# Probes of a segment mean sent as pieces of two rows between the data tiles

One core of a Trainium2 chip. The metric is the device time of one execution in microseconds (us). A profile's span is some 1.8 us shorter than the time of the same run.

## The reference

```python
def setup_inputs():
    n = 10_000_000
    num_segments = 10000
    return {
        "data": np.random.randn(n).astype(np.float32),
        "segment_ids": np.sort(np.random.randint(0, num_segments, n)),
    }

def reference(data, segment_ids):
    num_segments = int(segment_ids.max()) + 1
    sums = np.zeros(num_segments, dtype=np.float32)
    counts = np.zeros(num_segments, dtype=np.float32)
    np.add.at(sums, segment_ids, data)
    np.add.at(counts, segment_ids, 1)
    return sums / np.maximum(counts, 1)
```

The ids are sorted and a segment has about 1000 elements, so a piece of 875 neighbours rarely holds more than one boundary between segments.

## The kernel before

The 10 million elements are laid out as 128 partitions of 78125. A partition is cut into 90 rows of 875. In each row the kernel must find the position of the boundary, if there is one, and split the row's sum there.

It does not read all the ids. Every 175th id is read as a **probe** (five per row, each a transfer element of its own, 8 bytes). A **first look** (VectorE) finds between which two probes the boundary lies. A **gather** (issued by GpSimd) fetches the 175 ids there. Their sum (ScalarE, `add_ids`) gives the exact position in the **second look** (VectorE). Then VectorE sums the part of the row in front of the boundary (`split`) while ScalarE sums the whole row (`total`). The work goes in groups of six rows. These are the parts that matter here; bodies are cut where marked.

```python
L, S, K = 875, 175, 5            # row, distance of probes, probes per row
GROUPS = [6] * 15
X_PROBE, X_DATA, X_LOOK = 11, 26, 9
RING = 18                        # rows of gathered ids that fit

def load_probes(g):
    a = 0 if g == 0 else K * bounds[g] + 1
    b = min(K * bounds[g + 1] + 1, NPR)
    nc.sync.dma_start(out=pr_flat[:, a:b], in_=ids_p[:, a * S : (b - 1) * S + 1 : S])

def load_data(t):                # a tile is two rows; 18 buffers
    d = dpool.tile([P, 2 * L], FP32, name="data_t")
    ...
    nc.sync.dma_start(out=d[:, 0 : c - a], in_=data_p[:, a:c])

def first_look(g):               # five small VectorE steps
    ...                          # v.tensor_reduce(out=SG[:, a:b], in_=pr32[:, a:b, ...]) and so on
    gather(g)                    # six indirect transfers, one per row

def add_ids(r):                  # ScalarE; runs six rows ahead of total(r)
    nc.scalar.activation(out=junk_a[:, 0:W], in_=gt32[:, r % RING, ...], func=ACT.Copy, accum_out=GS[:, r : r + 1])

# where the steps are put: behind the split of row r on VectorE
put(a - 1, second_look(a, b))                             # just ahead of its group
put(max(bounds[g] - X_LOOK, 0), first_look(g), 5)         # nine rows ahead of its group

# the order of the data queue, and the main loop
for r in range(-X_PROBE - X_DATA, NR):
    while pnext < NG and bounds[pnext] <= r + X_PROBE + pnext // (NG - 1) + X_DATA:
        load_probes(pnext)
        pnext += 1
        if pnext == 1:
            load_data(0)
            nt = 1
    while nt < NT and 2 * nt <= r + X_DATA:
        load_data(nt)
        nt += 1
    ...
    while r >= -1 and gs < NR and gs <= r + x_sum(gs):
        add_ids(gs)
        gs += 1
    if r >= 0:
        total(r)
        split(r)
        for f in after[r]:
            f()
```

Probes and tiles share one queue, issued by SyncE and served in order. In the long run it reads: one group of probes (30 per partition, 3840 elements of 8 bytes), three tiles, one group of probes, and so on. Gathers have a queue of their own on the same 16 DMA engines.

## Time and profile before

| | kernel before |
|---|---|
| time, median of 3 | 189.86 us (189.63 to 189.91) |
| profiled run | 192.2 us |
| busy: VectorE, ScalarE, GpSimd | 140.9, 136.5, 99.8 us |
| VectorE's waits for data tiles | 6.0 us, 6 waits |
| ScalarE's waits for gathers | 37.0 us, 22 waits |
| last full tile landed (from the trace) | 176.0 us |

The profiled run was 2.3 us slower than the median, so its absolute times have to be taken with care. A second profile of the same kernel, among the experiments, took 190.58 us with a span of 188.7, and its last full tile landed at 174.5 us. Below, "before" in comparisons of traces is this second one.

A word on reading: the DMA share of a window is the time in which packets were open, summed over engines. Two queues on one engine, or a packet that is open but waits for its bytes, both raise it, so it can pass 1.00 and hides losses. The GB/s beside it is the safer column.

Three words recur. A **burst** is one group's probes on end in the queue. A **hold** is the time for which an issue instruction of the sync engine does not finish. A **descriptor** is one element of a transfer as one DMA engine sees it: a piece of two rows is 81 of them per engine (80 probes and one that tells of completion), a tile 9.

### The profile page before, as it was taken

The page shows a single profiled execution, that of the slowest core. Times are in us where ns is not written, and L with a number is a line of the kernel's source. Part 1 is how long each engine was busy: PE and PEld are TensorE (multiplying, and loading weights), DVE is VectorE, ACT ScalarE, POOL GpSimd, SP SyncE. Part 2 cuts the span into 40 slices and gives each one's busy share as a digit, 9 for nine tenths or more (in the row PEclk, how much of TensorE's full clock was granted, in tenths as well). Part 3 has the DMA queues.
Part 4 walks back from the last instruction along what each step waited for, and adds up shares of the span by engine and source line. Part 5 has one row for each costly group of instructions (what it writes and reads, how often), then busy time and mean ns, then how long its engine had stood idle before and what let it go on. Part 6 is the DMA issues. An engine that isn't in the chain of part 4 may idle for free.

```text
span 190.2 us, 1434 instructions
## 1 busy us (share of the span) xinstructions
PE 1.6 (1%) x6; PEld 1.4 (1%) x6; DVE 140.9 (74%) x438; ACT 136.5 (72%) x362; POOL 99.8 (52%) x119
## 2 busy tenths in 40 slices
PE   0000000000002000000000000000000000010000
PEld 0000000000001000000000000000000000010000
DVE  6521295969478792956978999566899969999991
ACT  8011498995989499698685948959868594999930
POOL 5577875065753737266272572726638278782000
DMA  6999999999999999999999999999999999999100
GB/s 29 174 188 414 271 330 413 174 405 261 331 412 176 401 284 297 412 147 374 311 284 408 138 370 339 266 392 186 401 301 274 299 349 412 397 405 399 54 0 8
DMA packets 70163, 54.61 MB, mean 287 GB/s; under 512 B 60016, under 2 KB 60584, under 8 KB 70151
## 3 DMA queue, kind: packets, MB, share of 16 engines
q1 hardware_dynamic: 64219, 40.50, 73.0%
q0 software_dynamic: 5760, 14.01, 23.2%
q14 instruction: 12, 0.10, 0.2%
q10 hardware_dynamic: 172, 0.00, 0.1%
HBM read 56.59 MB, written 0.04 MB: 298 GB/s over the span
## 4 chain that ended last, share of the span: by engine, by line
DMA 45%; issue 27%; ACT 9%; POOL 8%; DVE 7%; POOLq 0%; ACTq 0%; DVEq 0%
DMA GT<-in_segment_ids_dram,IDX 23%; DMA data_t<-in_data_dram 22%; POOL GT L304 7%; ACT junk_a L334 5%; ACT junk_a L314 4%; DVE junk_v L339 2%; DVE jj L235 1%; POOL i_i L197 0%; POOLq L304 0%; DVE most L744 0%; DVE add L736 0%; DVE PS L561 0%; DVE add L744 0%; DVE ps L558 0%; DVE most L750 0%
## 5 line engine op out<-in xcount | busy, mean ns | idle before, releaser
L304 POOL DMA_INDIRECT GT<-in_segment_ids_dram,IDX x90 | 90.9, 1010 | 70.1 <-ACT junk_a L314 28.1
L339 DVE SCALAR_TENSOR_TENSOR junk_v<-iota,q,data_t 128x875 bf16<-128x875 f32 x90 | 100.4, 1116 | 7.4 <-DMA data_t<-in_data_dram 6.0
L334 ACT ACTIVATE junk_a<-data_t 128x875 bf16<-128x875 f32 x90 | 83.6, 929 | 3.5 <-ACT junk_a L314 0.7
L314 ACT ACTIVATE junk_a<-GT 128x175 bf16<-128x175 int32 x90 | 32.4, 361 | 41.9 <-DMA GT<-in_segment_ids_dram,IDX 37.0
L321 DVE SCALAR_TENSOR_TENSOR q<-YY,GS 128x6 f32<-128x6 f32 (+1 forms) x19 | 3.2, 171 | 27.1 <-ACT junk_a L314 18.2
L314 ACT ACTIVATION_READ_ACCUMULATOR junk_a<-GT 128x1 f32 x90 | 16.8, 186 | 0.0
L334 ACT ACTIVATION_READ_ACCUMULATOR junk_a<-data_t 128x1 f32 x90 | 16.8, 186 | 0.0
L339 DVE DVE_READ_ACCUMULATOR junk_v<-iota,q,data_t 128x1 f32 x90 | 7.4, 82 | 0.0
L271 DVE TENSOR_REDUCE SG<-pr 128x6 f32<-128x30 int32 x15 | 2.7, 180 | 5.4 <-DMA pr<-in_segment_ids_dram 5.3
L186 ACT ACTIVATE GT<-q 128x3150 int32<-128x3150 f32 x1 | 3.0, 2998 | 0.0
L280 DVE TENSOR_SCALAR far<-ST 128x6 f32<-128x6 f32 x15 | 2.6, 171 | 0.5
L287 DVE SCALAR_TENSOR_TENSOR IDX<-ST,wb 128x6 int32<-128x6 f32 (+2 forms) x16 | 2.6, 165 | 0.5
L274 DVE SCALAR_TENSOR_TENSOR ST<-pr,SG 128x6 f32<-128x6 int32 x15 | 2.5, 165 | 0.5
L283 DVE TENSOR_TENSOR ST<-ST,far 128x6 f32<-128x6 f32 x15 | 2.5, 165 | 0.5
L290 DVE SCALAR_TENSOR_TENSOR YY<-ST,SG 128x6 f32<-128x6 f32 x15 | 2.4, 158 | 0.0
L235 DVE CAST jj<-jj_i 128x128 f32<-128x128 int32 x1 | 1.5, 1484 | 0.7 <-POOL jj_i L234 0.7
L186 ACT ACT_TABLE_LOAD x1 | 1.3, 1283 | 0.7 <-PEq L894 0.7
L703 POOL TENSOR_SCALAR pb<-pb 128x168 f32<-128x168 f32 (+1 forms) x2 | 1.6, 784 | 0.2
L589 DVE TENSOR_TENSOR_SCAN FFP<-NBP,FFP,XX 128x16 f32<-128x16 f32 (+2 forms) x4 | 1.5, 382 | 0.0
L543 PE MATMUL badp<-bads,ones 128*128 128x1 f32 x2 | 0.6, 362 | 106.3 <-DVE bads L542 106.3
L583 DVE TENSOR_TENSOR q<-T,q 128x44 f32<-128x44 f32 (+3 forms) x4 | 0.7, 180 | 0.9 <-DVE RB L574 0.4
L736 POOL TENSOR_TENSOR xa<-pa,RG 128x528 f32<-128x528 f32 x1 | 1.2, 1247 | 0.2 <-DVE RG L733 0.2
(129 smaller groups left out, 44.3 us busy)
## 6 DMA issues: line engine op xcount, KB each, us to landing
data_t<-in_data_dram SPq DMA_DIRECT2D x44, 875.0 KB
GT<-in_segment_ids_dram,IDX POOLq DMA_INDIRECT x90
data_t<-in_data_dram SPq DMA_DIRECT2D x1, 437.5 KB
pr<-in_segment_ids_dram SPq DMA_DIRECT2D x13, 30.0 KB
data_t<-in_data_dram SPq DMA_DIRECT2D x1, 125.0 KB
out_dram<-OUT SPq DMA_DIRECT2D x1, 36.6 KB
pr<-in_segment_ids_dram SPq DMA_DIRECT2D x1, 31.0 KB
pr<-in_segment_ids_dram SPq DMA_DIRECT2D x1, 26.0 KB
```

Of the source, the lines that this page charges most:

```text
L186: nc.scalar.activation(out=gt32[:, :, 0 : 2 * W : 2], in_=view(q5[:, 0, 0:1], [[0, RING], [0, W]]), func=ACT.Copy)
L235: nc.vector.tensor_copy(out=jj, in_=jj_i)
L271: v.tensor_reduce(out=SG[:, a:b], in_=pr32[:, a:b, 0 : 2 * K : 2], axis=AX.X, op=ALU.add)
L274: v.scalar_tensor_tensor(out=ST[:, a:b], in0=VI[:, a + 1 : b + 1], scalar=float(K), in1=SG[:, a:b], op0=ALU.mult, op1=ALU.subtract,)
L280: v.tensor_scalar(out=far, in0=ST[:, a:b], scalar1=0.0, scalar2=FAR, op0=ALU.is_equal, op1=ALU.mult)
L283: v.tensor_add(out=ST[:, a:b], in0=ST[:, a:b], in1=far)
L287: v.scalar_tensor_tensor(out=IDX[:, c:d], in0=ST[:, c:d], scalar=float(w), in1=wb[:, c:d], op0=ALU.mult, op1=ALU.add)
L304: nc.gpsimd.indirect_dma_start(out=GT[:, r % RING, :], out_offset=None, in_=ids2d[:], in_offset=bass.IndirectOffsetOnAxis(ap=IDX[:, r : r ...
L314: nc.scalar.activation(out=junk_a[:, 0:W], in_=gt32[:, r % RING, 0 : 2 * W : 2], func=ACT.Copy, accum_out=GS[:, r : r + 1],)
L321: nc.vector.scalar_tensor_tensor(out=KK[:, a:b], in0=YY[:, a:b], scalar=float(S // K), in1=GS[:, a:b], op0=ALU.mult, op1=ALU.subtract,)
L334: nc.scalar.activation(out=junk_a[:, 0:n], in_=d, func=ACT.Copy, accum_out=t)
L339: nc.vector.scalar_tensor_tensor(out=junk_v[:, 0:n], in0=iota[:, 0:n], scalar=KK[:, r : r + 1], in1=d, op0=ALU.is_lt, op1=ALU.mult, accum_ ...
```

## The change

The probes of a group go out as three transfers of two rows, with a tile between one piece and the next. The last piece of a group stands where the whole group stood, so the first look has its probes no later than before. The intent is to take the long run of small elements apart, so that the data queue never has 240 of them on end in front of a tile.

```diff
-X_PROBE = 11
+X_PIECE = 15
+PIECE = 2
...
-    def load_probes(g):
-        a = 0 if g == 0 else K * bounds[g] + 1
-        b = min(K * bounds[g + 1] + 1, NPR)
+    def load_probes(r0, r1):
+        a = 0 if r0 == 0 else K * r0 + 1
+        b = min(K * r1 + 1, NPR)
...
-    for r in range(-X_PROBE - X_DATA, NR):
-        while pnext < NG and bounds[pnext] <= r + X_PROBE + pnext // (NG - 1) + X_DATA:
-            load_probes(pnext)
-            pnext += 1
-            if pnext == 1:
+    for r in range(-X_PIECE - X_DATA, NR):
+        while pnext < NR and pnext <= r + X_PIECE + pnext // bounds[NG - 1] + X_DATA:
+            n = GROUPS[0] if pnext == 0 else PIECE
+            load_probes(pnext, pnext + n)
+            if pnext == 0:
                 load_data(0)
                 nt = 1
+            pnext += n
```

## The prediction

> **What bounds the kernel now.** I read the page first (busy shares, slices, queues), then who waited for whom, then the chain of work that ended last, then the sync engine's part of the timeline, and last windows around one burst of probes. On the page:
>
> ```profile
> DVE  6521295969478792956978999566899969999991
> ACT  8011498995989499698685948959868594999930
> DMA  6999999999999999999999999999999999999100
> GB/s 29 174 188 414 271 330 413 174 405 261 331 412 176 401 284 297 412 147 374 311 284 408 138 370 339 266 392 186 401 301 274 299 349 412 397 405 399 54 0 8
> q1 hardware_dynamic: 64219, 40.50, 73.0%
> q0 software_dynamic: 5760, 14.01, 23.2%
> ```
>
> The 16 DMA engines look full until about 175 us of 190.2, but the bytes swing between about 412 GB/s and dips of 138 to 188. A dip comes once per group: 57216 of the 64219 packets on q1 are 8-byte probes, 30 per partition and group. So the transfers are one bound. They are not the only one:
>
> ```profile
> ACT junk_a L314 <- DMA GT<-in_segment_ids_dram,IDX: 37.0, 22, 8.6
> ...
> DVE q L321 <- ACT junk_a L314: 18.2, 8, 3.6
> ...
> DVE junk_v L339 <- DMA data_t<-in_data_dram: 6.0, 6, 1.9
> ```
>
> VectorE waits only 6.0 us for data, all of it after 88 us (rows 38, 44, 50, 56, 68, 72). Its larger wait is for ScalarE's sums of gathered ids, and ScalarE waits 37.0 us for gathers. The chain alternates between the two:
>
> ```profile
> 59.67 7.07 DMA GT<-in_segment_ids_dram,IDX
> ...
> 85.58 13.21 DMA data_t<-in_data_dram
> ...
> 119.86 7.37 DMA GT<-in_segment_ids_dram,IDX
> ...
> 155.22 19.10 DMA data_t<-in_data_dram
> ```
>
> The gather part is a loop, read off the timeline. After the second look of group g (63.12 us) VectorE does four rows (4.9 us), then the first look of g+2 (68.01); 1.75 us later the first gather of g+2 is issued (69.76). A gather's sum runs 6.3 to 8.3 us after its issue, and six rows at ScalarE's pace of 1.54 us lead to the next second look (85.86). Two groups take 22.7 us, or about 11 us per group. The measured mean is (85.9 - 22.4) / 6 = 10.6 us up to 85.9 us, with no data wait at all, and (143.6 - 85.9) / 5 = 11.5 us after it, where the data waits lie.
>
> **What a burst of probes costs today.** Windows of the burst at 57 us (start:end, span, then busy us of each engine; the last two columns are the DMA share and GB/s):
>
> ```profile
> 57.00:60.00 3.00, 0.59 (x3) 0.63 (x4) 2.86 (x12) 2.90 (x8) 0.33 (x1) 1.00 1.23 155
> 60.00:61.00 1.00, 0.39 (x3) 0.30 (x2) 0.96 (x3) 0.97 (x3) 0.69 (x2) 1.00 0.90 154
> 61.00:67.00 6.00, 0.00 (x0) 0.00 (x0) 4.36 (x16) 3.19 (x10) 4.78 (x5) 1.00 0.99 389
> ```
>
> The second line is the interesting one: the probes are done at 60.2 us, yet the next 1 us moves 154 GB/s where 389 follow. The share of 0.90 hides this, because the first data packets after a burst are open for long without moving. The cause shows in the sync engine's issues:
>
> ```profile
> 84.78 0.70 SPq L162 DMA_DIRECT2D pr<-in_segment_ids_dram  x1
> ...
> 85.58 10.04 SPq L170 DMA_DIRECT2D data_t<-in_data_dram  x1
> ```
>
> The data tile behind each group of probes is held at issue 9.4 to 10.8 us, in eleven of the twelve groups sent from 12 us on (7.4 us in the last), even for tiles whose buffer was never used before; so it isn't a buffer. It is let go only when the probes ahead are nearly drained (holds end at 36.33, 59.58 and 83.72 us, the last probes of these bursts start 0.58, 0.55 and 0.75 us later, but for a straggling engine at 37.4). Its first packet starts 0.6 us later, its sixteenth 1.0 to 1.3 us later. Engines that had finished their probes are starved meanwhile. At 83.72 us one engine alone still had 99 probes to start while 15 had posted their completion; I read this as room for about 100 to 128 descriptors per engine between the issue and the data movers (an estimate). From the bytes of each 3 us window after a burst, taking 7000 bytes at 266 ns and a probe at 9 ns, the lost time is 0.5 to 1.3 us per burst, some 10 us in all.
>
> **What the skill says.** The Trainium skill, "DMA: Bandwidth & Descriptors", section "Rules for kernel authors", says that a strided last dimension becomes one descriptor per element, and that many small transfers should be joined, those under 64 KB being mostly overhead. The first agrees (57216 packets of 8 bytes). The second speaks against the change: 30 KB transfers become 10 KB. In "Queues, rings and completion order" the page says that an engine alternates between queues packet by packet; the trace agrees: where a gather is active, probes fall from 544 starts in 0.2 us (all 16 engines) to under 100. In "Latency and other measured facts" it gives about 0.6 us to the first byte on this path; the trace shows the same 0.6 us between the end of a hold and the first packet. That latency matters only when nothing is queued ahead of it.
>
> **The change part by part.** Removed: 14 issues of 26 or 30 probes per partition. Added: 42 of 10 (the last is shorter), so 28 issues more. At 0.65 us each (median of L162) they cost SyncE 18 us, off the path: it holds still about 10 us of every 12 anyway. VectorE's first look depends on three transfers instead of one; such a wait is 21 ns where it stands alone in this trace, 2 x 14 x 21 ns = 0.6 us at most. Completion packets: 28 x 16 of about 9 ns over 16 engines, 0.25 us. Probes and bytes are unchanged, and the last piece of a group is where the whole group was, so no first look starts later for it (first looks wait 5.3 us for probes, all before 14 us).
>
> Moved: per engine a piece is 80 probes and a completion, 81 descriptors, and a tile 9. Together 90, which fits into the 100 to 128 estimated above, where 241 did not. So the tile behind a piece should be queued before the piece starts, and most of the next piece while the tile takes its 2.1 us (8 packets of 266 ns). The starved 0.5 to 1.3 us should shrink to a fraction. I take 0.7 us off each of 13 bursts, or 9 us less transfer time, with the last data landing near 166 us instead of 175.
>
> What reaches the end is less. Only waits for data can shrink: of the 6.0 us, 0.5 + 1.9 + 0.6 us (rows 44, 56, 68) lie on the loop that leads from the second look at 75.0 us to ScalarE's last wait at 159.4; the wait of 1.5 us before row 72 partly runs beside it. From 159.4 ScalarE runs without a pause to 183.2 and the end follows 3 us later, so a gain ahead of 159.4 passes through whole. That is 3.0 + about 0.7 = 3.7 us. Against it: gathers now have uncontested engines during the starved gaps, and will share them with data instead. A sum starting 0.1 us later per gather loop over some 7 two-group loops costs 0.7 us; waits above, 0.3 us. Sum: 189.86 - 3.7 + 1.0 = 187.2, which I round to 187.0.
>
> **Rivals.** (a) Room for only about 64 descriptors: then each tile waits behind its piece as it does behind a group today and there are three gaps for one, up to 2 x 13 x 0.8 = 20 us more transfer time. For it: holds that end 0.55 us before a burst ends fit about 60 probes at 9 ns. Against it: the 99 probes on one engine at 83.72 us, and 81 on average per engine at the hold's end at 151.75. Time 195 to 205; I give it one in ten. (b) The transfers are the true bound from end to end: the chain gives them 45% and they run at 0.99 share. Then all 9 us come back: 181. Against it: the loop takes 10.6 us per group even before 85 us, where data is never late, and there earlier data gains nothing. (c) The gathers are slowed more than I allow, since the gaps close in their favour no longer: 0.4 us per loop would cost 3 us and give 189 to 190. For it: a sum follows its gather's issue by 4 us where the first gather meets a burst (row 48: 4.0, row 54: 3.6) and by about 7 where it meets data (row 30: 7.2). This is the most serious one.
>
> **Range and chances.** Between (b) in part and (c): 183.0 to 191.5. The line of 2% is 186.06, just below my value. Faster by over 2% 0.33, within 2% 0.55, slower by over 2% 0.12, of which most is (a).
>
> **What would show it.** Right: the GB/s row has no dips under 230 after 20 us, the 10 us holds of L170 become many short ones, VectorE's wait for data falls under 2 us, the data queue ends before 170 us, and ScalarE's wait for gathers stays at 34 to 41 us. The step on room is wrong if a low-byte gap follows every piece. The step on the loop is wrong if ScalarE's wait for gathers changes by more than 5 us, or if the end moves as far as the last data does.

## The result

The changed kernel took 188.80 us (188.19 to 189.03, 4 runs); the kernel before, in the same rounds, 189.88 (189.63 to 190.22). The ratio is 0.9937, with a 95% interval from 0.9907 to 0.9966. Ratios here are the mean time of one kernel's fast runs over that of the other's of the same rounds, so they are not quite the ratio of the medians quoted. The result is correct.

187.0 us was forecast, so the time lies inside the range, but the gain is 1.1 us where the working gave 2.7 (189.86 to 187.2, which was rounded to 187.0). The profile of the changed kernel is that of its quickest run (188.19 us, span 186.4). Its page, slices of the span with GB/s:

```profile
DMA  6999999999999999999999999999998999999000
GB/s 28 178 178 340 331 325 328 306 341 330 316 330 319 338 333 305 326 335 332 314 310 335 318 328 317 329 344 307 326 246 246 343 405 406 405 406 391 15 0 12
```

The same row of the second profile of the kernel before:

```profile
GB/s 28 176 141 386 357 244 403 231 308 395 212 406 247 351 394 236 407 208 407 311 280 402 189 392 292 268 390 219 401 284 292 283 347 415 401 404 398 63 0 9
```

The dips are gone: from the fourth slice to the last probes, before swung between 189 and 407, and now the queue runs at 305 to 344 GB/s, with one exception, two slices of 246 at 135 to 144 us. Who waited for whom:

```profile
ACT junk_a L315 <- DMA GT<-in_segment_ids_dram,IDX: 35.9, 24, 6.4
...
DVE q L322 <- ACT junk_a L315: 21.7, 10, 6.9
DVE junk_v L340 <- DMA data_t<-in_data_dram: 6.7, 12, 0.8
```

And in the second profile of the kernel before:

```profile
ACT junk_a L314 <- DMA GT<-in_segment_ids_dram,IDX: 38.1, 23, 8.1
...
DVE q L321 <- ACT junk_a L314: 25.0, 10, 7.6
...
DVE junk_v L339 <- DMA data_t<-in_data_dram: 7.3, 6, 2.0
```

The waits for data did not go away. They are twice as many and shorter (0.8 us at most, where it was 2.0), and in sum 6.7 us. Sync engine's issues in the timeline (start, duration, what):

```profile
65.98 2.46 SPq L171 DMA_DIRECT2D data_t<-in_data_dram  x1
68.49 0.68 SPq L163 DMA_DIRECT2D pr<-in_segment_ids_dram  x1
69.21 2.57 SPq L171 DMA_DIRECT2D data_t<-in_data_dram  x1
```

One hold of ten microseconds per group has become one of 2 to 5 us per tile, which is about the pace at which the queue drains a tile and a piece. And the chain:

```profile
57.77 6.46 DMA GT<-in_segment_ids_dram,IDX
...
103.30 6.19 DMA GT<-in_segment_ids_dram,IDX
...
111.47 7.40 DMA data_t<-in_data_dram
...
129.50 10.82 DMA data_t<-in_data_dram
...
160.93 6.87 DMA GT<-in_segment_ids_dram,IDX
```

Data takes 10% of it and gathers 23%; in the second profile of the kernel before they take 16 and 27%, in the first 22 and 23%. The last full tile landed at 171.8 us, 2.7 us before the 174.5 of the kernel before. The 2.7 us are themselves unsure: they compare a run of 188.19 us with one of 190.58, and in a kernel further down (g3_only, a run of 188.32 us) this tile lands at 171.8 us with a single group in pieces. But the gaps did close, and the transfers did not end 9 us earlier. That is the first thing to explain.

**Why closed gaps gave so little.** Five windows of the changed kernel have nearly no gather in them; three of them (columns as in the prediction):

```profile
69.00:72.00 3.00, 0.00 (x0) 0.00 (x0) 1.64 (x5) 2.87 (x9) 2.39 (x3) 1.00 1.11 321
81.00:84.00 3.00, 0.00 (x0) 0.00 (x0) 1.66 (x6) 2.88 (x9) 2.23 (x3) 1.00 1.09 314
114.00:117.00 3.00, 0.00 (x0) 0.00 (x0) 1.50 (x4) 2.87 (x9) 2.39 (x3) 1.00 1.10 313
```

All five together (57 to 60, 69 to 72, 81 to 84, 114 to 117, 126 to 129) last 15 us; the tiles in them move 312 GB/s, with the probes it is 317. At 7000 bytes per 266 ns on each of 16 engines (421 GB/s) the bytes need 11.1 us. The other 3.9 us went to 403 probes per engine, counted in the trace: 9.6 ns each. In the fastest stretches of a burst of the kernel before, with probes queued and no gather beside them, 544 probes started per 0.2 us, which is 5.9 ns each on an engine. So, as an estimate from these fastest stretches, a group's 240 probes cost 240 x 5.9 ns = 1.4 us and a gap before, and 240 x 9.6 ns = 2.3 us without a gap after. A whole burst is not that fast: with gathers beside it for a part of its time, its middle 90% took 2.07 us on average. Over the whole stretch from 20 us to the last probe, gathers and tiles both taken at 26 bytes per ns and engine, all else counted to the probes, six rows cost 2.84 us before and 2.72 after. The saving is 0.1 us per group by this count, where I had taken 0.7. The count differs between profiles of one kernel (the first profile of the kernel before gives 3.0 us), so the saving may be 0.1 to 0.3 us, but not 0.7.

### The profile page after: what moved, and what is told of

It reads as the page before. It is cut to its first block, busy times and chain, and to the rows that moved or that the text cites. A ratio compares the mean times of both kernels' runs of the same rounds, so it can differ in the third digit from the quotient of the medians.

```text
span 186.4 us, 1479 instructions
## 1 busy us (share of the span) xinstructions
PE 1.6 (1%) x6; PEld 1.4 (1%) x6; DVE 140.8 (76%) x438; ACT 136.6 (73%) x362; POOL 99.9 (54%) x119
## 4 chain that ended last, share of the span: by engine, by line
DMA 33%; issue 32%; ACT 14%; POOL 13%; DVE 4%; POOLq 1%; ACTq 0%
DMA GT<-in_segment_ids_dram,IDX 23%; POOL GT L305 12%; DMA data_t<-in_data_dram 10%; ACT junk_a L335 9%; ACT junk_a L315 5%; POOLq L305 1%; DVE jj L236 0%; POOL i_i L198 0%; DVE junk_v L340 0%; DVE most L745 0%; DVE add L737 0%; POOL pb L703 0%; DVE sel L648 0%; DVE most L751 0%; POOL KL L689 0%
## 5 line engine op out<-in xcount | busy, mean ns | idle before, releaser
L315 ACT ACTIVATE junk_a<-GT 128x175 bf16<-128x175 int32 x90 | 32.4, 360 | 38.1 <-DMA GT<-in_segment_ids_dram,IDX 35.9
L236 DVE CAST jj<-jj_i 128x128 f32<-128x128 int32 x1 | 0.8, 840 | 0.7 <-POOL jj_i L235 0.7
L571 DVE RECIPROCAL ct<-ct 128x16 f32<-128x16 f32 (+2 forms) x4 | 1.2, 300 | 0.1
L544 PEld LDWEIGHTS badp<-bads,ones 128*128 128x128 f32 x2 | 0.5, 310 | 104.8 <-DVE bads L543 104.8
```

## The experiments

I had two theories. A: the loop of looks, gathers and sums holds the end, and eats what the transfers save. B: the transfers hold the end alone and save little. The edits are given against the kernel before or the changed kernel. The medians of the kernel before lay between 189.1 and 190.7 us (the chip was not always the same). Five of the experiments had slow executions (strict, after_look12, split_only and piece3 one each, after_early two of six, its profiled one among them); the ratios leave these out, the medians quoted contain them.

**A second profile of the kernel before** (no edit).

> The kernel before, unchanged, to get a profile in the fast state: the one that the prediction was read from took 192.2 us where the median is 189.9, and was marked slow. If the slow state made the gap between the two profiles (3.8 us of span) larger than the one between the medians (1.1 us), this profile shows a span near 188 and the last data landing 1 to 2 us earlier than the 176 us seen. If the profile was typical, the span is 190 again.

Measured: 190.58 us (one run, so its state is unknown), span 188.7, last full tile at 174.5, waits of VectorE for data 7.3 us, of ScalarE for gathers 38.1. So part of the distance between the first two profiles was the slow run. The shape was typical: dips down to 141 to 250 GB/s once per group.

**No two pieces in a row.**

```diff
-        while pnext < NR and pnext <= r + X_PIECE + pnext // bounds[NG - 1] + X_DATA:
+        while pnext < NR and pnext <= r + X_PIECE + X_DATA:
```

> The changed kernel, but the pieces of the last group come one row later, so that no two pieces follow each other (in the changed kernel two do, near 135 to 140 us, and 1.2 to 1.8 us of transfer time are lost there). Theory (room for about 100 descriptors per engine, gaps where probes exceed it): the low stretch at 138 to 141 us disappears, no window of 3 us between 20 and 145 us moves under 240 GB/s, and the last data land 1 to 1.5 us earlier. Time: if transfers set the end, 187.4 (1.3 us less than the changed kernel); if the loop of gathers sets it, 188.6 to 188.9, the same.

Measured: 188.48 us (188.28 to 188.80 for the five fast runs; the sixth was slow at 191.27), ratio 0.9936 [0.9891, 0.9980]. Windows of the changed kernel and of this one around the place where two pieces followed each other:

```profile
138.00:141.00 3.00, 0.00 (x0) 0.00 (x0) 2.96 (x8) 2.81 (x9) 2.39 (x3) 1.00 0.83 110
```

```profile
138.00:141.00 3.00, 0.00 (x0) 0.00 (x0) 2.95 (x5) 2.83 (x8) 2.39 (x3) 1.00 1.03 305
```

The hole is filled. Two pieces on end, 162 descriptors per engine, bring a gap; one piece and a tile do not. But the last full tile landed only 0.6 us earlier (171.2; 1 to 1.5 were expected) and the time is the same: the better end of the queue did not reach the end of the kernel.

**The loop relieved, first try.** In both kernels first looks and probes were moved three rows ahead: `first_look(g)` put at `max(bounds[g] - X_LOOK - 3, 0)`, and `X_PROBE` 14 or `X_PIECE` 18.

> The kernel before with the first look, and so the gathers, of groups 3 to 13 three rows earlier, and the probes three rows earlier too, so that the loop of looks, gathers and sums has some 3.6 us more room per two groups. Theory A (the loop holds the end, the transfers hold it second): ScalarE's wait for gathers falls from 37 us to under 20 us, VectorE's wait for data rises over 10 us, time 186.5 to 188.5. Theory B (the transfers hold the end alone): time within 0.6 us of before, 189.3 to 190.5, with waits only moved from gathers to data.

> The changed kernel with first looks and probes three rows earlier. Theory A (the loop eats the transfer time that the change saves): with the loop out of the way the whole saving shows, 3 to 5 us under the same edit of the kernel before, 183 to 185. Theory B (transfers hold the end alone, and the change saves little of them): 188 to 189, about 1 us under the same edit of the kernel before.

Measured: before with it 190.98 us, ratio 1.0080 [1.0026, 1.0133]; changed kernel with it 190.76, ratio 1.0002 [0.9933, 1.0071]. ScalarE's wait for gathers fell to 16.1 and 15.7 us, VectorE's for data rose to 24.2 and 24.4, and ScalarE, which had hardly waited for data, now did for 22.4 and 23.3. Both times lie above what either theory had forecast. The waits only moved from gathers to data, which is nearer to theory B. But the edit also put more probes in front of the first tiles, so it is not clean.

**Less data.** In both kernels a tile is loaded without its last 125 columns, and the second row is read 125 columns earlier. All sums keep their size; the result is wrong.

```diff
-        nc.sync.dma_start(out=d[:, 0 : c - a], in_=data_p[:, a:c])
+        c2 = c - 125 if t < NT - 1 else c
+        nc.sync.dma_start(out=d[:, 0 : c2 - a], in_=data_p[:, a:c2])
...
-        d = tiles[r // 2][:, (r % 2) * L : (r % 2) * L + n]
+        o = (r % 2) * (L - 125 if r < NR - 2 else L)
+        d = tiles[r // 2][:, o : o + n]
```

> The kernel before with 1/14 less data moved: each tile of two rows is loaded without its last 125 columns (6500 bytes per partition for 7000), and the second row is summed from column 750 on instead of 875. All sums keep their sizes, probes and gathers are untouched; the result is wrong on purpose. If the transfers hold the end: 8 packets x 44 tiles x 19 ns (1/14 of 266 ns) = 6.7 us less, 182 to 184 us, and the span still ends 14 to 15 us after the last full tile. If the loop of looks, gathers and sums holds it: at most 1.5 us less, 188 to 189.6.

> The changed kernel with the same 1/14 less data (wrong result on purpose). Transfers hold the end: 6.7 us under the changed kernel, 181 to 183, and still about 1 us under the same cut of the kernel before. Loop: 187 to 188.8.

Measured: before with less data 188.75 us (188.15 to 189.21), ratio 0.9950 [0.9895, 1.0005]; changed with less data 186.73 (186.35 to 187.06), ratio 0.9841 [0.9788, 0.9894]. In the kernel before the last full tile landed at 167.4 us, 7.1 us earlier than at 174.5, and the end moved by 0.9 us. Its waits, with no wait for data among them:

```profile
ACT junk_a L315 <- DMA GT<-in_segment_ids_dram,IDX: 36.9, 21, 7.8
DVE q L322 <- ACT junk_a L315: 29.0, 10, 7.5
```

So theory B falls as well: with no wait for data left, the loop alone takes nearly as long. And here the two kernels are 2.0 us apart, with no overlap of their runs, though VectorE and ScalarE wait for data in neither. The changed kernel's 186.73 us lie just under the 187 to 188.8 that were forecast for a loop that holds the end. Its waits:

```profile
ACT junk_a L316 <- DMA GT<-in_segment_ids_dram,IDX: 28.9, 19, 4.2
DVE q L323 <- ACT junk_a L316: 27.8, 10, 6.7
...
ACT junk_a L316 <- DVE IDX L289: 6.4, 1, 6.4
```

**Both reliefs, and a cleaner one.** First looks three rows earlier, probes left where they were.

```diff
-            put(max(bounds[g] - X_LOOK, 0), first_look(g), 5)
+            put(max(bounds[g] - X_LOOK - 3, 0), first_look(g), 5)
```

> The kernel before with the first looks of groups 3 to 13 three rows earlier, probes where they were. Theory (two bounds of nearly one height: with less data the kernel before still took 188.75 us, so its loop alone gives about that, and the transfers alone give about 189): VectorE's wait for data rises over 12 us, time 188.5 to 190.5. Rival (the loop was the one bound, and the earlier probes spoiled the first try at this): 186 to 187.5.

> The changed kernel with the same edit. Two bounds: 186.5 to 188.5 (its last data land some 3 us earlier than before's, so the transfers alone would give 186 to 187), VectorE's wait for data over 10 us. Rival: 184 to 185.5.

> Both reliefs at once in the kernel before: 1/14 less data (wrong result on purpose) and first looks three rows earlier. Two bounds of one height: each relief alone gave 1 us or nothing, both give at least 4 us, 181 to 185. Rival (a third thing, the pace of ScalarE and VectorE themselves, holds the end): as with the cut alone, 188 to 189.

> Both reliefs at once in the changed kernel. Two bounds: 179 to 183, at least 3 us under the cut alone (186.7). Rival (pace of the engines): 186 to 187.

Measured, with the earlier runs, as ratios to the kernel before of the same rounds (median of all runs in us, 95% interval):

| | kernel before | changed kernel |
|---|---|---|
| as it is | 1 | 0.9937 (188.80) [0.9907, 0.9966] |
| less data | 0.9950 (188.75) [0.9895, 1.0005] | 0.9841 (186.73) [0.9788, 0.9894] |
| earlier looks | 0.9870 (187.74) [0.9790, 0.9950] | 0.9886 (188.42) [0.9808, 0.9963] |
| both | 0.9596 (182.94) [0.9515, 0.9677] | 0.9626 (182.91) [0.9550, 0.9703] |

The forecast for the kernel before with earlier looks was missed: 187.74 us lies under the 188.5 to 190.5 of two bounds and nearer to the 186 to 187.5 of the loop as the one bound, and VectorE's wait for data is 7.6 us and not over 12 (ScalarE's is 19.6). The other three of these four runs lie in the ranges of two bounds, and it is the row with both reliefs that speaks for them.

Three things can be read from the table. Less data alone gives the kernel before half a per cent, earlier looks alone 1.3, both 4: there are two bounds of nearly one height, and lifting one uncovers the other. With the looks earlier, the two kernels can't be told apart, with all data as well as with less: in the mean of the fast runs the changed kernel is 0.3 us slower with all data (give or take 0.9, an estimate from their scatter) and 0.2 us slower with less. With less data and the looks where they were, they are 1.1% apart. So what the change wins there, it wins in the loop, and its saving of transfer time does not show where transfers matter most.

Why not? I compared the 1.2 us after a burst in five bursts of the kernel before, without and with earlier looks. Without:

```profile
72.40:73.60 1.20, 0.00 (x0) 0.00 (x0) 0.00 (x0) 1.17 (x3) 0.90 (x2) 1.00 0.98 160
83.70:84.90 1.20, 0.00 (x0) 0.00 (x0) 0.85 (x2) 1.17 (x4) 0.91 (x1) 1.00 0.99 172
```

With:

```profile
73.00:74.20 1.20, 0.00 (x0) 0.00 (x0) 0.00 (x0) 1.14 (x5) 0.00 (x0) 1.00 1.05 286
84.30:85.50 1.20, 0.00 (x0) 0.00 (x0) 0.00 (x0) 1.14 (x5) 0.00 (x0) 1.00 1.03 248
```

The mean of the five is 183 GB/s without and 292 with. By packets, over all twelve bursts, gathers move about 107 GB/s in this time without and 213 with; data 60 and 44. With the looks earlier, gathers are under way when the tile behind the probes is late, and use the engines. Six rows of probes then cost 2.63 us by the count above, about as the pieces' 2.72. A gap that other traffic fills is no loss, and closing it is no gain.

One thing goes against calling this a loop set free. VectorE's waits for probes, without and with earlier looks:

```profile
DVE SG L271 <- DMA pr<-in_segment_ids_dram: 5.8, 2, 4.4
```

```profile
DVE SG L271 <- DMA pr<-in_segment_ids_dram: 17.7, 9, 4.7
```

Without the edit, each first look from group 3 on starts at least 5.7 us after the last probe of its group; with it, eight of the twelve start 0.6 to 0.9 us after it, seven of them having waited 1.0 to 2.1 us. So the earlier looks relieve the loop only up to the point where their own probes hold it, and what it waits for then is a transfer again.

**The split without the alternation.** In the kernel before each group goes out as three transfers, one directly after the other:

```diff
-        nc.sync.dma_start(out=pr_flat[:, a:b], in_=ids_p[:, a * S : (b - 1) * S + 1 : S])
+        for c in range(a, b, 2 * K) if g else [a]:
+            e = min(c + 2 * K, b) if g else b
+            nc.sync.dma_start(out=pr_flat[:, c:e], in_=ids_p[:, c * S : (e - 1) * S + 1 : S])
```

> The kernel before with each group's probes sent as three transfers of two rows directly after each other, at the old place: the split without the alternation. Theory (what counts is how many probes stand between two tiles, 243 descriptors per engine here as before): dips in GB/s once per group as before, last tile and time as before within 0.7 us, 189.0 to 190.3. Rival (shorter transfers are cheaper in themselves, or each transfer costs a gap of its own): 188.4 with the first, over 192 with the second.

Measured: 193.87 us, ratio 1.0234 [1.0178, 1.0291]. I missed this; the rival with a gap for each transfer (over 192 us) was right. I had taken the number of probes between two tiles to be all that counts. The trace shows a second gap inside the burst: probe starts fall from 441 in the 0.2 us at 94.4 us to between 22 and 114 from 94.8 to 95.8 us, before the third piece starts in earnest at 96.0, and from 118.6 to 119.6 us it is the same. The middle of a burst (from 5 to 95% of its probes) takes 3.0 us on average instead of 2.07. The third piece's own issue was held until 95.1 us. I read it so: an issue that is held waits for the transfer ahead, and only then runs into the 0.6 us to its first packet. A piece of 80 probes drains in 80 x 5.9 ns = 0.5 us (an estimate) and does not cover that; a tile, 2.1 us, does. So the alternation is what makes small pieces bearable, and the split is a cost.

**Pieces of three rows** (`PIECE = 3`, `X_PIECE = 14`).

> The changed kernel with two pieces of three rows per group (15 probes per partition, 121 descriptors per engine, and 9 of the tile: 130). Room for 100 to 128 descriptors: the pair doesn't fit, a part of the gap comes back twice per group, 189.0 to 190.0. Rival (each piece costs the same small gap of about 0.3 us however long it is, and the pieces of two rows have three of them per group): one fewer per group, 12 x 0.3 = 3.6 us less transfer time than the changed kernel, 185 to 187.5.

Measured: 189.56 us, ratio 0.9982 [0.9913, 1.0051]; eight of the slices between 20 us and the last probe fall to 262 to 284 GB/s, where the changed kernel stays over 300 but for the two of 246. The rival with one small gap per piece is out (it wanted 185 to 187.5). It fits the estimate of room for 100 to 128 descriptors, but the interval includes the changed kernel's ratio.

**Where in the kernel the gain is made.** The lead of the changed kernel over the kernel before, both with less data, is there at row 6 (its split starts at 30.4 us, before at 31.5) and hardly grows after it (row 84: 168.9 and 170.1). From this I formed the theory that the gain is made at the start, where the first gathers meet pieces and tiles in turn and not three tiles on end. Four kernels with all data, two with less. The edit chooses which groups go in pieces:

```diff
-        while pnext < NR and pnext <= r + X_PIECE + pnext // bounds[NG - 1] + X_DATA:
-            n = GROUPS[0] if pnext == 0 else PIECE
+        def piece():
+            return PIECE if 6 <= pnext < 24 else 6      # start_only
+            #      PIECE if pnext >= 24 else 6          # rest_only
+            #      PIECE if 18 <= pnext < 24 else 6     # g3_only
+
+        while pnext < NR and pnext <= r + X_PIECE + PIECE - piece() + pnext // bounds[NG - 1] + X_DATA:
+            n = piece()
```

with groups that are not in pieces at their old place in the queue.

> Pieces of two rows for groups 1 to 3 alone; from group 4 on each group's probes are one transfer at the old place. Theory (the gain is made at the start): the split of row 0 starts at 21.4 to 21.9 us (before: 22.2 to 22.6) and that of row 6 before 30.8 us (before: 31.2 to 31.9), bursts and dips later as before, time as the changed kernel, 0.6 to 1.5 us under before. Rival (the gain comes from the pieces all along): time within 0.4 us of before.

> The other half of the change: groups 1 to 3 as before, pieces of two rows from group 4 on. Theory: row 0 at 22.2 to 22.6 us, row 6 after 31.2, GB/s flat after 25 us, time within 0.5 us of before. Rival (pieces all along): the gain of the changed kernel, 0.8 us or more under before.

> Only group 3 in pieces of two rows, between tiles 1 to 4; all other groups as before. If it is the alternation with tiles 1 to 3 that lets the first gathers land sooner: row 0 at 21.4 to 22.0 us, row 6 before 30.9, time 0.5 to 1.5 us under before. If it is the shorter transfers of groups 1 and 2: row 0 at 22.2 or later, time within 0.4 us of before.

> start_only with the first looks of groups 3 to 13 three rows earlier. If the start gain is one of the loop and transfers hold the end once the loop is relieved: as the kernel before with early looks, a ratio of 0.984 to 0.990 to before. If the two add up: 0.975 to 0.982.

Measured: start_only 190.35 us, ratio 1.0059 [1.0015, 1.0104]; rest_only 189.32, 1.0013 [0.9964, 1.0061]; g3_only 188.96, 0.9998 [0.9962, 1.0033]; start_only_early 187.48, 0.9924 [0.9883, 0.9965]. The early lead was there in part (the split of row 0 at 21.6 us in start_only and 21.3 in g3_only, 22.6 before) and brought nothing at the end: by row 30 start_only stood at 74.9 us, where before had 74.5. The theory of the start fell for the kernel with all data. So did its rival: neither half gave the whole change's gain by itself. start_only_early missed both of its forecasts (0.984 to 0.990 and 0.975 to 0.982). Two more, with less data, where the difference is clean:

> Pieces for groups 1 to 3 alone, with 1/14 less data (wrong result on purpose). If the loop's gain is made at the start: a ratio of 0.982 to 0.988 to before, like the changed kernel with this cut (0.984), row 6 before 30.8 us and the lead kept to the end. If it is made by the pieces later on: 0.992 to 0.998, like the kernel before with this cut (0.995), with an early lead at row 6 that is lost by row 30.

> Pieces from group 4 on alone, with 1/14 less data (wrong result on purpose). Gain made at the start: 0.992 to 0.998 of before. Gain made later on: 0.982 to 0.988. If both this run and the other lie between 0.987 and 0.992, each half gives a part.

Measured: start_only_cut 188.02 us (187.22 to 188.44), ratio 0.9891 [0.9842, 0.9940]; rest_only_cut 186.57 (186.16 to 187.78), ratio 0.9825 [0.9774, 0.9875]. With the whole change it was 0.9841, with none 0.9950. So the pieces from group 4 on give the loop's gain, all of it within the noise. The start gives 1.1 us by the ratios (0.9891 against 0.9950, from different calls); their intervals overlap and don't separate it from nothing. The last full tile tells the same: 164.1 us with the later pieces (163.8 with the whole change), 167.4 with the pieces at the start alone (167.4 with none). Nor was the lead at row 6 a mark of the start: with less data and the later pieces alone that row's split starts at 30.6 us, where it is 31.5 with no pieces.

## Why the prediction was right and wrong

**Right: the gaps, and how they close.** The GB/s row is flat, the ten-microsecond holds became short ones, and the one place where two pieces meet shows the gap again; putting a tile between them takes it away.

**Wrong: "I take 0.7 us off each of 13 bursts, or 9 us less transfer time, with the last data landing near 166 us instead of 175."** This is the step that failed, and it is a term of wrong size. The last full tile moved by 2.7 us with all data (174.5 to 171.8) and by 3.6 us with less (167.4 to 163.8), which is 0.2 to 0.3 us per burst. I had priced every probe at 9 ns, in bursts and in pieces alike, and taken the whole gap as gain. The kernel before starts queued probes 5.9 ns apart at its fastest; pieces between tiles cost 9.6 ns per probe. Six rows went from 2.84 to 2.72 us in all. That the slower probes eat most of the gap is worked out from these counts, and no experiment changed the one without the other. That gathers use the gap is read from the packets.

**Wrong: the 3.7 us from waits for data.** They were to fall under 2 us and stayed at 6.7, as twelve short ones. With the transfers hardly quicker, I see nothing that would have taken them away.

**Right: that a loop holds the end beside the transfers.** With 1/14 less data the kernel before gained 0.9 us of the 6.7 us that left the queue. Rival (b), the transfers as the one bound, is out; so is its opposite, since earlier looks alone gave only 1.3%. The two are coupled, and both have to go (4%). One sign that I had named against this step, the end moving as far as the last data does, is nearly there in the two profiles: the last tile moved by 2.7 us and the span by 2.3 (188.7 to 186.4). But the medians moved by 1.1, and with less data the kernel before shows the two apart: 7.1 us for the last tile and 0.9 for the end.

**Wrong in sign: gathers that run slower after the change, 0.7 us against it.** With less data, where VectorE and ScalarE wait for no data, the changed kernel was 2.0 us shorter. With all data no slowing shows: ScalarE's wait for gathers is 38.1 us before and 35.9 after, and the median time from a gather's issue to its sum 7.37 and 7.11 us (7.50 in the first profile of the kernel before, so little can be read from the size). I take the 1.1 us measured to be of this kind, and not of the kind that I had worked out, since no gain shows with the looks earlier; that is a reading and not shown. Rival (c) is out with it, and so is (a), three gaps for one; the split without alternation shows what (a) would have looked like.

**Open.** How the later pieces shorten the loop is not shown: with less data the median time from a gather's issue to its sum is 7.25 us before and 7.13 after, which is too little to read a cause from. Nor is it shown why, with all data, rest_only stayed at 1.0013 while the whole change gave 0.9937 in rounds of its own and 0.9936 in the form without double pieces; these are differences of under 1%. Why a piece's probes take 9.6 ns and not 5.9 between tiles is open too.

No combination with the change beat the kernel before with its first looks three rows earlier (187.74 us, ratio 0.9870, correct; the 187.48 us of start_only_early came in a call in which the kernel before took 189.13): it is the lowest ratio of a correct kernel here, though the interval reaches 0.9950 and the changed kernel with the same edit (0.9886) can't be told from it.

## What to carry to other kernels

When a queue shows a hole behind a run of small elements, price the hole and the run together, per element and all in, before counting the hole as gain: smoothing can slow the run by what it saves in the hole. Ask also whether another queue would use the hole. And where two bounds are of nearly one height, lift each alone and both together on the chip before you believe either; here the three answers were 0.5, 1.3 and 4%.

## What the Trainium skill lacked or had wrong

- "DMA: Bandwidth & Descriptors", section "Rules for kernel authors", advises to join small transfers, those under 64 KB being mostly overhead. Alone, splitting 30 KB into three of 10 KB cost 2.3%, in line with it. With a tile of 875 KB between the pieces it cost nothing (ratio 0.9937). The rule does not speak of what stands behind a transfer in its queue.
- "Perfetto Trace Analysis", section "DMA Instruction — HWDGE (DVE, Sync)", says that an issue lasts until all its descriptors have been generated, and that their buffer can fill up. It gives neither the size of that buffer nor how long an issue is held. On the sync engine's queue the runs show 9.4 to 10.8 us behind 241 descriptors per engine, 2 to 5 us behind 81, with the first packet 0.6 us after the hold. One engine had 99 probes left when a hold ended, from which I estimate room for about 100; no run fixes the upper end of 128 in the prediction.
- "DMA: Bandwidth & Descriptors", section "Bandwidth", gives about 10.5 ns per packet for a transfer of 64 packets issued from GpSimd, which is not a time on one engine. It has no time per small element in a long queued run from the sync engine. There the runs show 5.9 ns per 8-byte element on an engine in the fastest stretches of a burst, and 9.6 ns in pieces between tiles.
